# A hybrid encoder layer: mixer work emitted by an estimated clock of each engine, and modulation weights asked for three tiles ahead in four buffers

## The chip, the core and the metric

The kernel runs on one core of one Trainium2 chip. The metric is the device time of one execution in microseconds (us), lower is better. The core has five engines with instruction queues of their own, each worked off in order: TensorE (PE in the profile, with its weight loads as PEld), VectorE (DVE), ScalarE (ACT), GpSimd (POOL) and SyncE (SP), which here issues nearly all DMAs. The kernel is written in a tile framework: the Python code emits instructions in some order, and the framework turns that order, with priorities, into the order of each engine's queue and adds the semaphores. So the order in which the Python code emits is what the programmer controls.

## What is computed

One layer of a streaming encoder in float32 on 512 prompt frames and 64 sample frames, width 2048. Each step is matrix products with large weights, with small recurrent work between:

```python
mod = silu(c) @ w_ada + b_ada                        # 2048 -> 6 x 2048: sh1, sc1, g1, sh2, sc2, g2
h = rmsnorm(x, norm1) * (1 + sc1) + sh1
proj = h @ w_in                                      # split into columns of two groups of heads
o_a = GLA(q, k, v, low-rank gate)                    # 4 heads: S_t = diag(a_t) S_{t-1} + k_t v_t^T
o_b = GDN(silu(conv4(q, k, v)), beta, alpha)         # 8 heads: S_t = a_t (I - b_t k_t k_t^T) S_{t-1} + b_t k_t v_t^T
x = x + g1 * (concat(norm(o_a) * silu(r), norm(o_b) * silu(g)) @ w_out)
h = rmsnorm(x, norm2) * (1 + sc2) + sh2
x = x + g2 * (silu(conv3(gate) + b) * val) @ w_down  # gate, val = h @ w_up
y = rmsnorm(x, final_norm)
```

Each recurrence is evaluated in blocks; for GDN a block needs the inverse of a unit lower triangular matrix, `(eye + lower)`. The states of the recurrences and convolutions are outputs too.

## The kernel before

Products in float32 are made of three passes over a high and a low part of weight and activation (`split` makes the parts on ScalarE, L662, and VectorE, L663; `mm6` is the six matmuls of one 128-row tile for two halves of the frames, L565 and L567).

The stages are: `head` (norms, the first two modulation parts, some early projections), the mixer stage, the rest of `w_out`, `up`, `down`. The change lies in the mixer stage. There the main stream is a sequence of projection tiles (`in_tile`: 16 times `mm6`), 31 for the GDN heads and 19 for the GLA heads, followed by half of `w_out` (16 tiles of 8). After each `mm6` comes one `tick`, 928 in all. A tick does three things:

- `run_due` runs what was put off by a count of ticks (`later`);
- `job_step` resumes the jobs, Python generators in a list: `gdn` for each of eight heads and for the samples, `gla` for each of four heads and for the samples. It goes through them in order and stops after the first that emitted something; a job that says WAIT only lets a tick pass;
- with a rate of `ADA_RATE` = 0.72 a tick it resumes `ada_blocks`, which computes the other four modulation parts: 16 blocks of 8 weight tiles (512 KB each, loaded by L900), each tile four VectorE operations (L938), and at the end of a block a small sum on TensorE (`ada_sum`, L910).

A job has to leave time between an instruction on one engine and the next instruction that needs its result on TensorE, because TensorE's queue is in order: what is emitted too early makes it stand. Before, this time is a fixed count of ticks for each place (`rest(REST_S)`, `hop` with two ticks of rest, `LAG_CONV`, `LAG_COPY` for results of convolutions and copies). The steps that the prediction names:

- `gdn` computes decays (ScalarE; GpSimd `affine_select`), sums of squares and their `rsqrt` (VectorE add L151, GpSimd power), `a` = masked k k^T (L228), and then calls `inverse16`: it stores `a` to DRAM (L373), loads its 16x16 diagonal blocks onto 32 partitions (L379), inverts them with 28 GpSimd operations (listed under L1812, the helper that records GpSimd's operations), stores the result (L390), loads it spread out (L394) and masks it on VectorE (L399). Then come the levels that build the inverse up (matmuls L250, L256, L265, L270, each with a VectorE operation after it), and four blocks of states (L288 to L317). Operations of jobs on VectorE and ScalarE carry the line L1797 of their helper, which gives them a precedence of 80 places.
- `gla` has seven levels (L442 and operations around it), a transpose, and four blocks (L479 to L485).
- `gdn_conv` runs the short convolution (L1073 to L1083); its results are transposed in jobs (L158).
- `ada_blocks` has three buffers `aw` and asks for a tile two tiles ahead.

Buffers named `m` are a common pool of 15. `xr` is a pair of buffers used at the start for the first projection and constants of `narrow`, and later for the loads of `w_out`'s stage. `K.drain()` emits what is left of the jobs after the first half of `w_out`, and the loop behind it what is left of the modulation.

Of the kernel before, what the change touches and what calls it, by code (L numbers as in the profile page):

```python
# [16 lines left out]
P = 128  # L17
# [85 lines left out]
class Kern:  # L103
    def __init__(self, tc, ctx, i, o):
        self.tc, self.nc, self.ctx, self.i, self.o = tc, tc.nc, ctx, i, o
        self.n = 0
        self.cp = ctx.enter_context(tc.tile_pool(name="cp", bufs=1, side="left"))
        self.pg = ctx.enter_context(tc.tile_pool(name="pg", bufs=2, space=PSUM))
        self.c, self.scrap = {}, []
        self.jv, self.ja = _Sooner(tc, tc.nc.vector), _Sooner(tc, tc.nc.scalar)  # L110
        self.pool = _InTurn(tc, tc.nc.gpsimd)
# [37 lines left out]
    def rsqrt(self, out, src, n, parts=P):  # L149

        self.nc.vector.tensor_scalar_add(out[:parts, :n], src[:parts, :n], EPS)  # L151
        self.pool.tensor_tensor(out[:parts, :n], out[:parts, :n], self.mhalf[:parts, :n], op=ALU.pow)

    def transpose4(self, src4, n=4):

        ps = self.bank()
        for b in range(n):
            self.nc.tensor.transpose(ps[:, b * P:(b + 1) * P], src4[:, b], self.c["ident"])  # L158
# [10 lines left out]
    def gdn(self, qF, kF, x, gain, hcols, gb, s0, s_out, o_put, last_level):  # L169
# [11 lines left out]
        V, A, T = self.jv, self.ja, nc.tensor  # L181
# [4 lines left out]
        yield from self.rest(REST_C)  # L186
# [12 lines left out]

# [7 lines left out]

        self.rsqrt(kt[:, 0], ss, 4)
# [3 lines left out]
        V.tensor_tensor(kt[:, 1], kt[:, 1], nbeta, op=ALU.mult)  # L212
        for b in range(4):
            A.activation(dl[:, b], dl[:, b], AF.Copy, scale=kt[:, 1, b:b + 1])
        yield
# [4 lines left out]
        self.rsqrt(rq, ss, 4)  # L220
        V.tensor_scalar_mul(rq, rq, float(P) ** -0.5)
        yield from self.rest(REST_T)


# [6 lines left out]

# [42 lines left out]
        while not self.ready(x, "v"):  # L274
            yield WAIT
# [7 lines left out]
        for b in range(4):  # L283
            parts = [(0, P, st)] if not pair else [(0, 64, s0[2 * b]), (64, P, s0[2 * b + 1])]
            if parts[0][2] is not None:
# [5 lines left out]
                yield from self.hop(0)  # L291
# [6 lines left out]
            yield from self.hop(0)  # L298
# [20 lines left out]
            yield from self.hop(0)  # L319
# [7 lines left out]
        self.rsqrt(rr, ss, 4)  # L327
        for b in range(4):
            A.activation(ops[:, b], ops[:, b], AF.Copy, scale=rr[:, b:b + 1])
        yield from self.rest(REST_N)  # L330
        fps = self.transpose4(ops)
        A.activation(kF, fps, AF.Copy, scale=gain)
        while not self.ready(x, "gate"):
            yield WAIT
        V.tensor_tensor(kF, kF, x["gate"](), op=ALU.mult)
        yield from self.rest(REST_O)
        o_put(kF)

    def ready(self, x, name):

        return name in x and self.ticks >= x.get((name, "at"), 0)

    def put_ready(self, x, name, get, lag):

        x[name], x[name, "at"] = get, self.ticks + lag
# [7 lines left out]
    def rest(self, n):  # L353

        for _ in range(n):
            yield WAIT

    def hop(self, n=REST_H):

        yield  # L360
        yield from self.rest(n)

    def inverse16(self, a, work):
# [16 lines left out]
        yield from self.rest(REST_D)  # L380
# [8 lines left out]
        yield from self.rest(REST_S)  # L389
        nc.sync.dma_start(d1.rearrange("w q f -> q w f"), lane)  # L390
        yield from self.rest(REST_L)
# [4 lines left out]
        yield from self.rest(REST_X)  # L396
        t, u = self.m4(), self.m4()
        for w, x in enumerate((t, u)):
            nc.vector.tensor_tensor(x.rearrange("p b (n j) -> p b n j", n=8), cm[:, w].unsqueeze(2).to_broadcast(sh),  # L399
                                    c["bd16"].rearrange("p (n j) -> p n j", n=8).unsqueeze(1).to_broadcast(sh), op=ALU.mult)  # L400
        yield from self.rest(REST_U)
        return u, t

    def gla(self, nb, qF, kF, g, x, s0, s_out, o_put):
# [7 lines left out]
        V, A, T = self.jv, self.ja, nc.tensor  # L412
        pair = s0 is not None
        w = nb * P
        at = self.m()[:, :w].rearrange("p (b t) -> p b t", b=nb)
# [5 lines left out]
        for s in LEVELS:  # L421
# [10 lines left out]
            A.activation(e, e, AF.Exp, scale=1.0 / 16.0)  # L432
            e3 = e.rearrange("p (b t) -> p b t", b=nb)
# [5 lines left out]
            yield from self.rest(REST_G)  # L439
            ps = self.bank()  # L440
            for b in range(nb):
# [8 lines left out]
        A.activation(qd, g, AF.Exp, scale=1.0 / 16.0)  # L450
        V.tensor_tensor(qd, qd, qF, op=ALU.mult)
# [5 lines left out]
                        gs[:, :, seg - 1:seg].to_broadcast([P, nseg, seg]), gs, op=ALU.subtract)  # L457
        A.activation(kd, kd, AF.Exp, scale=1.0 / 16.0)
        kd3 = kd.rearrange("p (b t) -> p b t", b=nb)
# [4 lines left out]
        yield  # L464
        yield from self.rest(REST_V)
        A.activation(kT, self.transpose4(kd3, nb), AF.Copy)
        yield from self.hop()
        while not self.ready(x, "v"):
            yield WAIT
# [4 lines left out]
        for b in range(nb):  # L474
# [22 lines left out]
            if b % 2 == 1:  # L497
                self.rsqrt(rr[:, b - 1:b + 1], ss[:, b - 1:b + 1], 2)
                V.tensor_tensor(ons[b // 2], ops, self.col4(rr[:, b - 1:b + 1], 256), op=ALU.mult)
            yield  # L500
        if not pair:
            nc.sync.dma_start(s_out, st)
        yield from self.rest(REST_N)
        for f in range(2):
# [4 lines left out]
            yield  # L509
        for f in range(2):  # L510
            dst = (qd, kd3)[f]
            while not self.ready(x, f"gate{f}"):
                yield WAIT
            V.tensor_tensor(dst, dst, x[f"gate{f}"](), op=ALU.mult)
        yield from self.rest(REST_O)
# [4 lines left out]
    def later(self, n, f):  # L520

        self.due.append((self.ticks + n, f))

    def run_due(self):
        while self.due and self.due[0][0] <= self.ticks:
            self.due.pop(0)[1]()

    def tick(self):

        self.ticks += 1  # L530
        self.run_due()
        self.at_job += JOB_RATE
# [3 lines left out]
        self.at_ada += ADA_RATE  # L536
        while self.at_ada >= 1:
            self.at_ada -= 1
            next(self.ada, None)

    def job_step(self):
        for g in list(self.jobs):
            r = next(g, self)
            if r is self:
                self.jobs.remove(g)
# [3 lines left out]
    def drain(self):  # L549
        while self.jobs:  # L550
            self.ticks += 1
            self.run_due()
            self.job_step()
# [1322 lines left out]
```

## Time and profile before

| | |
|---|---|
| runs | 2917.21, 2911.84, 2914.27 us; median 2914.27 |
| profiled execution | 2915.48 us, of which span 2913.8 us |
| TensorE busy in the span | 2823.6 us (97%) |
| mixer stage | about 186 to 1125 us |
| TensorE busy in 186 to 1125 us | 894.1 of 939.0 us |
| granted TensorE clock, mean of the span | 0.985 of full |

The profile is of one execution. Busy time of TensorE is modelled at its end, so it tells where TensorE stood still rather than how fast it was. The row of a group or wait gives the line, the engine, tiles (out<-in), a count, and times; "idle before" is the time an engine stood still ahead of such an instruction and what ended it. A line can be that of a helper (L1797 for VectorE and ScalarE in jobs, L1812 for GpSimd).

### The profile page before, as it was taken

Reading aid. Unit: us, or ns where it says so; the run is one execution under the profiler, and the core shown is the slowest. Engines: PE = TensorE matmul, PEld = TensorE weight load, DVE = VectorE, ACT = ScalarE, POOL = GpSimd, SP = SyncE. Lnnn points to the kernel's source line nnn. Section 1 sums busy time; section 2 is a strip of 40 time slices with the busy share of each in tenths; the row PEclk is TensorE's granted clock in tenths of the full one; section 3 lists DMA queues with packets and bytes.
Section 4 is the critical chain, followed back from the end, with each engine's and each line's share of the span. In section 5 each row is a group of like instructions: output and inputs, shape, how many; then the busy total and the mean of one; then the engine's idle time right before and its main releaser. Section 6 shows DMA issues by size and latency. Waiting matters only on the chain.

```text
span 2913.8 us, 52011 instructions
## 1 busy us (share of the span) xinstructions
PE 2823.6 (97%) x20964; PEld 2739.5 (94%) x20964; DVE 2055.0 (71%) x3305; ACT 1183.4 (41%) x2030; POOL 306.1 (11%) x513
## 2 busy tenths in 40 slices
PE   6997989999899999999999999999999999999998
PEld 3787989999899998999999999999999999999997
DVE  3467667777568687578888888888888855555555
ACT  4143544555454343255444444444444522222223
POOL 0004141222200000000111111111111100000000
PEclk8998999999899999999999999999999999999999
DMA  8965444555445548633333333333333563333221
GB/s 301 307 173 154 138 134 138 152 155 159 132 122 150 150 128 229 181 115 97 115 108 101 107 103 114 108 100 107 108 110 107 165 201 97 119 98 117 83 82 66
DMA packets 535444, 395.53 MB, mean 136 GB/s; under 512 B 59657, under 2 KB 465412, under 8 KB 535204
## 3 DMA queue, kind: packets, MB, share of 16 engines
q1 hardware_dynamic: 527860, 390.54, 44.8%
q8 instruction: 165, 2.70, 0.4%
q10 hardware_dynamic: 7344, 1.67, 0.3%
q14 instruction: 75, 0.61, 0.1%
HBM read 356.47 MB, written 35.67 MB: 135 GB/s over the span
## 4 chain that ended last, share of the span: by engine, by line
PE 83%; DVE 6%; POOL 3%; issue 2%; DMA 2%; ACT 2%; SPq 0%; ACTq 0%; POOLq 0%; DVEq 0%
PE g L565 28%; PE g L567 14%; PE bank L1476 12%; PE bank L1475 11%; PE bank L1477 11%; POOL m L1812 2%; DVE acc L938 2%; PE bank L754 1%; PE bank L158 1%; PE bank L442 1%; DVE m L1797 1%; DVE wl L663 1%; DVE ca L1078 1%; ACT m L1797 0%; PE bank L256 0%
## 5 line engine op out<-in xcount | busy, mean ns | idle before, releaser
L1476 PE MATMUL bank<-slot,wh 128*128 128x290 f32 x2464 | 738.7, 300 | 0.0
L1475 PE MATMUL bank<-slot,wh 128*128 128x290 f32 x2464 | 734.7, 298 | 0.0
L1477 PE MATMUL bank<-slot,wl 128*128 128x290 f32 x2464 | 728.4, 296 | 0.0
L565 PE MATMUL g<-slot,wh 128*128 128x288 f32 x3168 | 551.4, 295 | 0.3 <-DVE slot L1245 0.3
L565 PE MATMUL g<-hh,wh 128*128 128x288 f32 x2048 | 478.6, 314 | 1.3 <-ACT wh L662 0.8
L1477 PEld LDWEIGHTS bank<-slot,wl 128*128 128x128 f32 x2464 | 471.5, 191 | 0.0
L1476 PEld LDWEIGHTS bank<-slot,wh 128*128 128x128 f32 x2464 | 468.5, 190 | 0.1
L565 PEld LDWEIGHTS g<-slot,wh 128*128 128x128 f32 x3168 | 464.1, 188 | 0.7 <-DVE slot L1245 0.5
L1475 PEld LDWEIGHTS bank<-slot,wh 128*128 128x128 f32 x2464 | 463.6, 188 | 0.1
L662 ACT ACTIVATE wh<-raw 128x1024 fp32r<-128x1024 f32 x215 | 227.6, 1059 | 538.5 <-PE g L565 513.7
L565 PE MATMUL g<-hl,wh 128*128 128x288 f32 x2048 | 444.9, 298 | 0.0
L567 PE MATMUL g<-hh,wl 128*128 128x288 f32 x2048 | 443.4, 298 | 0.0
L1245 DVE SCALAR_TENSOR_TENSOR slot<-g,mod,slot 128x512 f32<-128x512 f32 (+1 forms) x448 | 201.6, 491 | 263.8 <-PE g L567 262.7
L565 PEld LDWEIGHTS g<-hh,wh 128*128 128x128 f32 x2048 | 329.8, 192 | 25.5 <-issue 14.9
L938 DVE SCALAR_TENSOR_TENSOR acc<-aw,ct,acc 128x512 f32<-128x512 f32 x480 | 337.1, 748 | 19.5 <-DMA aw<-in_w_ada_dram 19.5
L567 PE MATMUL g<-slot,wl 128*128 128x288 f32 x1584 | 341.9, 294 | 0.0
L565 PEld LDWEIGHTS g<-hl,wh 128*128 128x128 f32 x2048 | 333.7, 191 | 3.6 <-issue 2.7
L567 PEld LDWEIGHTS g<-hh,wl 128*128 128x128 f32 x2048 | 331.0, 190 | 2.2 <-issue 2.0
L663 DVE TENSOR_TENSOR wl<-raw,wh 128x1024 fp32r<-128x1024 f32 x215 | 262.5, 1221 | 65.1 <-ACT wh L662 64.4
L1422 ACT ACTIVATE wh<-raw 128x1024 fp32r<-128x1024 f32 x176 | 186.1, 1057 | 224.8 <-PE bank L1476 189.5
L567 PEld LDWEIGHTS g<-slot,wl 128*128 128x128 f32 x1584 | 255.5, 188 | 0.0
L1423 DVE TENSOR_TENSOR wl<-raw,wh 128x1024 fp32r<-128x1024 f32 x176 | 215.2, 1223 | 54.8 <-ACT wh L1422 54.8
(355 smaller groups left out, 3101.0 us busy)
## 6 DMA issues: line engine op xcount, KB each, us to landing
raw<-in_w_up_dram SPq DMA_DIRECT2D x176, 512.0 KB
aw<-in_w_ada_dram SPq DMA_DIRECT2D x128, 512.0 KB
raw<-in_w_in_dram SPq DMA_DIRECT2D x100, 512.0 KB
raw<-in_w_down_dram SPq DMA_DIRECT2D x88, 512.0 KB
hraw<-in_w_ada_dram SPq DMA_DIRECT2D x64, 512.0 KB
raw<-in_w_out_dram SPq DMA_DIRECT2D x32, 512.0 KB
slot<-actd SPq DMA_DIRECT2D x44, 288.0 KB
actd<-v SPq DMA_DIRECT2D x44, 256.0 KB
```

The costliest lines, as they stand in the source:

```text
L565: T.matmul(ps[:, h if bank is None else bank, :n], wh, x[:, h, :n], start=f, stop=False)
L567: T.matmul(ps[:, h if bank is None else bank, :n], wl, ah[:, h, :n], start=False, stop=stop)
L662: nc.scalar.activation(hi[:, :n_], raw[:, :n_], AF.Copy)
L663: nc.vector.tensor_tensor(lo[:, :n_], raw[:, :n_], hi[:, :n_].bitcast(F32), op=ALU.subtract)
L938: V.scalar_tensor_tensor(acc[s], w[:, k], col, acc[s], op0=ALU.mult, op1=ALU.add)
L1245: self.nc.vector.scalar_tensor_tensor(x1[:, :, z], ps[:, :, c], gain[:, q:q + 1], x1[:, :, z], op0=ALU.mult, op1=ALU.add)
L1422: self.nc.scalar.activation(hi, src, AF.Copy)
L1423: self.nc.vector.tensor_tensor(lo, src, hi.bitcast(F32), op=ALU.subtract)
L1475: T.matmul(ps, wh[:, j], hi, start=(c < 3 and j == 0), stop=False, skip_group_check=True)
L1476: T.matmul(ps, wh[:, j], lo, start=False, stop=False, skip_group_check=True)
L1477: T.matmul(ps, wl[:, j], hi, start=False, stop=(j == NPAIR - 1), skip_group_check=True)
L1812: r = f(*a, **kw)
```

## The change

The ticks are replaced by a running estimate of time. `now` advances by `TICK_US` with each tick and by a fixed price for each TensorE instruction of a job. Every instruction of the stage on VectorE, ScalarE and GpSimd goes through a wrapper that adds its estimated duration to that engine's `free` time, and a job's own `chain` is the estimated end of its last step. A job waits until `now` has passed `chain` plus `HOP_US`. GpSimd's estimate has longer durations than the other two, and an extra for the power in `rsqrt`; a DMA counts `DMA_US` plus `ISSUE_US` for each transfer. Convolutions and the GLA gate become generators of their own (`tasks`), run at each tick. The modulation goes on as long as VectorE's estimated backlog is under `ADA_BACKLOG`; its waits don't use up its rate. Its tiles are asked for three ahead, in two buffers `aw` and the two `xr` in turn, but only one ahead and in `aw` alone from the last GLA head on (`ending`). The pool `m` has 17 buffers. Sample jobs and GLA jobs wait until at most one `gdn` job of a head is left (`fewer`).

```diff
-REST_S, REST_L, REST_D, REST_X, REST_U, REST_T, REST_H, REST_N, REST_O, REST_G = 2, 3, 6, 4, 12, 2, 2, 4, 4, 4
-REST_C = 11
-REST_V = 5
-LAG_CONV, LAG_COPY = 11, 5
-ADA_AHEAD = 2
+TICK_US, HOP_US, DMA_US, ISSUE_US = 0.795, 0.25, 2.6, 0.5
+ADA_BACKLOG, ADA_CREDIT = 1.0, 200.0
+OP_US = {"V": (0.12, 1 / 960.0), "A": (0.10, 1 / 960.0), "G": (0.45, 1 / 400.0)}
+ADA_AHEAD = 3
...
     def rsqrt(self, out, src, n, parts=P):
-        self.nc.vector.tensor_scalar_add(out[:parts, :n], src[:parts, :n], EPS)
+        self.tv.tensor_scalar_add(out[:parts, :n], src[:parts, :n], EPS)
         self.pool.tensor_tensor(out[:parts, :n], out[:parts, :n], self.mhalf[:parts, :n], op=ALU.pow)
+        self.slower("G", 0.7)
+    def rsqrt_steps(self, out, src, n):
+        self.rsqrt(out, src, n)
+        yield from self.until()
...
+    def charge(self, key, n, extra=0.0):
+        base, per = OP_US[key]
+        start = max(self.free[key], self.now + HOP_US, self.chain or 0.0)
+        self.free[key] = end = start + base + per * n + extra
+        if self.chain is not None:
+            self.chain = end
+    def charge_pe(self, us):
+        self.now += us
+        if self.chain is not None:
+            self.chain = max(self.chain, self.now)
+    def until(self):
+        while self.now < self.chain + HOP_US:
             yield WAIT
-    def hop(self, n=REST_H):
+    def hop(self):
         yield
-        yield from self.rest(n)
+        yield from self.until()
+    def moved(self, n=1):
+        self.chain = max(self.chain, self.now) + DMA_US + n * ISSUE_US
...
     def inverse16(self, a, work):
-        yield from self.rest(REST_S)
+        yield from self.until()
         nc.sync.dma_start(d0[:P * pitch].rearrange("(p f) -> p f", p=P), a.rearrange("p b t -> p (b t)"))
-        yield from self.rest(REST_L)
+        self.moved()
+        yield from self.until()
...
         for b in range(4):
             nc.sync.dma_start(xx[8 * b:8 * b + 8], blocks[:, :, b, :16])
-        yield from self.rest(REST_D)
+        self.moved(4)
+        yield from self.until()
...
         G.tensor_copy(xt, xx.rearrange("p i j -> p j i"))
-        yield from self.rest(REST_S)
+        yield from self.until()
         nc.sync.dma_start(d1.rearrange("w q f -> q w f"), lane)
-        yield from self.rest(REST_L)
+        self.moved()
+        yield from self.until()
...
-        yield from self.rest(REST_U)
+        yield from self.hop()
         return u, t
...
     def tick(self):
-        self.ticks += 1
+        self.now += TICK_US
         self.run_due()
+        self.run_tasks(list(self.tasks))
         self.at_job += JOB_RATE
         while self.at_job >= 1:
             self.at_job -= 1
             self.job_step()
-        self.at_ada += ADA_RATE
-        while self.at_ada >= 1:
+        self.at_ada = min(self.at_ada + ADA_RATE, ADA_CREDIT)
+        while self.at_ada >= 1 and self.free["V"] - self.now < ADA_BACKLOG:
+            r = next(self.ada, self)
+            if r is self or r is WAIT:
+                break
             self.at_ada -= 1
-            next(self.ada, None)
...
     def ada_blocks(self, blocks, accs):
-            while len(got) < min(len(todo), n + 1 + ADA_AHEAD):
-                got.append(self.ada_load(*todo[len(got)], lambda: self.ap.tile([P, 1024], F32, tag="aw", bufs=1 + ADA_AHEAD, name=self.name("aw"))))
+            while len(got) < min(len(todo), n + 1 + (1 if self.ending else ADA_AHEAD)):
+                j = len(got)
+                own = lambda: self.ap.tile([P, 1024], F32, tag="aw", bufs=2, name=self.name("aw"))
+                got.append(self.ada_load(*todo[j], self.xr if j % 2 and not self.ending else own))
                 if n == 0:
-                    yield
+                    yield WAIT
...
             if k0 + 2 == KD:
-                yield from self.rest(4)
+                yield from self.pause(self.free["V"] + HOP_US)
                 yield from self.ada_sum(blk, acc)
...
     def gdn_conv(self, ps, t, dst, name, h, done):
         A.activation(acc[:, :579], cb[:, 0:579], AF.Copy, scale=self.vec("gdn_conv_w", t))
+        yield from self.until()
         for j in range(1, 4):
             V.scalar_tensor_tensor(acc[:, :579], cb[:, j:j + 579], self.vec("gdn_conv_w", 24 * j + t), acc[:, :579],
                                    op0=ALU.mult, op1=ALU.add)
+        yield from self.until()
         A.activation(dst, acc[:, 0:512], AF.Silu)
+        done(end + HOP_US)
...
+class _Timed:
+    def __getattr__(self, name):
+        f = getattr(self.engine, name)
+        def g(*a, **kw):
+            out = kw["out"] if "out" in kw else a[0]
+            self.k.charge(self.key, _size(out), 0.2 if "accum_out" in kw else 0.0)
+            return f(*a, **kw)
+        return g
+class _TimedPE:
+    def transpose(self, out, *a):
+        self.k.charge_pe(0.11)
+        return self.engine.transpose(out, *a)
+    def matmul(self, out, *a, **kw):
+        self.k.charge_pe(0.22 * max(1.0, _size(out) / P))
+        return self.engine.matmul(out, *a, **kw)
...
-    BUFS = {"m": 15, "qkv": 8, "gt": 3}
+    BUFS = {"m": 17, "qkv": 8, "gt": 3}
```

In `gdn` and `gla` every `rest` and fixed `hop` becomes `until` or `hop`, and every wait for a convolution, copy or gate becomes `wait_for` an estimated time.

More of the change, by code (lines that the diff above doesn't have):

```diff
@@ L290, in gdn @@
                 rhs = r
-                yield from self.hop(0)
+                yield from self.hop()
             else:
@@ L549, in drain @@
     def drain(self):
-        while self.jobs:
-            self.ticks += 1
+        while self.jobs or self.tasks:
+            self.now += TICK_US
             self.run_due()
+            self.run_tasks(list(self.tasks))
             self.job_step()
@@ L1183, in gla_gate @@
             A.activation(t, t, AF.Ln, bias=one[:, 0:1])
+        self.slower("A", 2.6)
+        yield from self.until()
         for z, t, c0, n, seg in parts:
```

262 lines of the change are left out of this document (167 added, 95 removed).

## The prediction

> **What bounds the kernel now.** I read the page first (sections 1 and 4), then a table of windows over the mixer stage, then the list of what TensorE waited for, and last the timeline around one long gap.
>
> ```profile
> PE 2823.6 (97%) x20964; PEld 2739.5 (94%) x20964; DVE 2055.0 (71%) x3305; ACT 1183.4 (41%) x2030; POOL 306.1 (11%) x513
> PE 83%; DVE 6%; POOL 3%; issue 2%; DMA 2%; ACT 2%; SPq 0%; ACTq 0%; POOLq 0%; DVEq 0%
> 186.00:1125.00 939.00, 894.08 (x6704) 859.45 (x6703) 685.92 (x1307) 447.87 (x1035) 185.38 (x341) 0.97 0.52 148
> 437.00:729.00 292.00, 284.67 (x2217) 277.09 (x2216) 216.41 (x395) 146.81 (x371) 72.51 (x131) 0.99 0.53 151
> ```
>
> In the last two rows the columns are PE, weight load, DVE, ACT and POOL busy, then granted clock, DMA share and GB/s. TensorE bounds the kernel. The change only reorders the mixer stage (186 to 1125 us), where TensorE idles 939.0 - 894.1 = 45 us and the clock is below full. No TensorE instruction is removed, so idle time and clock there are all that can be won. The steady GDN heads (437 to 729) lose only 292.0 - 284.7 = 7 us; the losses are in single events.
>
> ```profile
> PE bank L256 <- POOL m L1812: 11.7, 2, 7.8
> PE bank L256 <- DVE m L1797: 9.3, 4, 7.5
> PE bank L250 <- DVE m L399: 6.0, 2, 3.2
> PE bank L158 <- ACT qkv L1082: 5.0, 2, 2.5
> PE bank L158 <- ACT qkv L1219: 3.3, 1, 3.3
> PE bank L270 <- DVE m L1797: 2.1, 1, 2.1
> ```
>
> Each row is total us, times, longest. The waits are few and long: the inverse levels L250, L256 and L270, and transposes waiting for a late convolution (L1082). One event in order of time shows how they arise:
>
> ```profile
> 264.29 16.14 POOL L1812 TENSOR_TENSOR m<-m 32x14 f32<-32x14 f32 x28
> 264.85 0.38 SPq L900 DMA_DIRECT2D aw<-in_w_ada_dram  x1
> 281.11 0.33 SPq L390 DMA_DIRECT2D d<-m  x1
> 281.48 0.42 SPq L900 DMA_DIRECT2D aw<-in_w_ada_dram  x1
> 285.64 0.75 DVE L938 SCALAR_TENSOR_TENSOR acc<-aw,ct,acc 128x512 f32<-128x512 f32 x1 [9.32 <-DMA aw<-in_w_ada_dram]
> 286.31 0.41 DVE L1797 TENSOR_TENSOR m<-bank,consts 128x256 f32<-128x256 f32 x1
> 286.88 1.94 PE L256 MATMUL bank<-m,m 128*128 128x64 f32 x8 [7.54 <-DVE m L1797]
> SPq L390 <- POOL m L1812: 85.3, 9, 15.7
> SPq L900 <- DVE acc L938: 229.4, 82, 11.5
> ```
>
> POOL works 16 us on a GDN inverse. Its result store (L390) stands at the head of SP's queue meanwhile, the next modulation tile behind it is asked for only at 281.48, DVE waits 9.3 us for that tile, and the level's own DVE operation stands behind. TensorE gets the bill. The store blocks SP in all nine jobs, 9.5 us each.
>
> The clock adds to it (PE busy, clock, DMA share, GB/s):
>
> ```profile
> 260.00:263.30 3.30, 3.30 (x26) 1.00 0.19 40
> 286.90:288.50 1.60, 1.60 (x8) 0.50 0.98 328
> 288.50:292.60 4.10, 4.10 (x19) 0.50 1.09 316
> 757.90:763.00 5.10, 5.10 (x23) 0.50 0.51 121
> ```
>
> After the 7.5 us gap TensorE works 5.7 us at half clock and loses 2.85; after the 3.3 us gap 5.1 us, losing 2.55. The 2.8 us wait at L250 just before 260 cost no clock. So a long gap costs its length and about 2.7 us more. [...]
>
> **The change part by part.**
>
> *Waits by the clock.* Fixed counts of ticks give way to waits until an estimated end. The gain is where counts went wrong: a `rsqrt` on POOL queued behind another job's inverse now enters the estimate, so DVE is no longer given work that blocks at its head, and the store L390 is emitted when POOL should be done. The estimate for one inverse is 28 operations at 0.45 us plus size/400 (15.4), memset 0.5 and copy 1.1: 17.0 us.
>
> ```profile
> L1812 POOL TENSOR_TENSOR m<-m 32x14 f32<-32x14 f32 (+6 forms) x252 | 115.1, 457 | 18.6
> 530.36 1.64 DMA d<-m
> 532.06 2.69 DMA cm<-d
> ```
>
> Measured: 28 x 0.457 = 12.8 us plus the copy, so the estimate is generous on average. The two DMA steps behind it are estimated at 3.1 + 3.6 = 6.7 us and took 4.4: some 2.3 us in hand, plus rounding to ticks. The waits this addresses are L256, L250, L270 and L158 from L1082: 11.7 + 9.3 + 6.0 + 2.1 + 5.0 = 34.1 us. Bounds of the gain: 34 if all go, 17 if half move to the next hop, since POOL's work itself is not shortened. I take nine tenths, 31, because all of these go back to late POOL, SP or DVE order, which the clock tracks. The 3.3 us (L1219, ACT) I leave. Four of these gaps are long (7.8 and 3.9 in the first row, 7.5, 3.2): 4 x 2.7 = 11 us of clock (0 to 14).
>
> *Shorter hops.* Before, a hop is three ticks (2.4 us at the 0.795 that the change's own constant gives a tick). After, it is the first tick past the estimated end plus 0.25 us, mostly two. About 24 hops in each of nine `gdn` jobs and 15 in each of five `gla` jobs make 290. What a hop loses today:
>
> ```profile
> PE bank L442 <- DVE m L1797: 0.7, 1, 0.7
> PE bank L295 <- DVE sq L1797: 0.5, 1, 0.5
> PE bank L507 <- DVE m L1797: 0.5, 1, 0.5
> L663 DVE TENSOR_TENSOR wl<-raw,wh 128x1024 fp32r<-128x1024 f32 x34 | 41.8, 1229 | 6.8 <-ACT wh L662 6.5 <-DMA qkv<-early_aq 0.2
> L1797 ACT ACT_TABLE_LOAD x18 | 23.1, 1283 | 0.7 <-ACT ts L1236 0.4
> ```
>
> Almost nothing: single waits of 0.5 to 0.7 us. With the slack cut, a hop behind a 1.23 us weight split can wait for part of it. Lower bound 0; upper 290 x 0.2 = 58 us, each hop waiting half of its own 0.41 us operation. I take 0.04 us, nearer to today's rows: one hop in fifteen waits 0.6. That is +12.
>
> *Modulation pace.* Rests no longer cost steps: 16 blocks x 32 = 512 steps at 0.72 a tick end after 711 ticks of 928, not 915.
>
> ```profile
> L938 DVE SCALAR_TENSOR_TENSOR acc<-aw,ct,acc 128x512 f32<-128x512 f32 x150 | 105.2, 746 | 0.0
> 437.00:729.00 292.00, 199.93 (x1082) 158.08 (x1082) 0.99 0.53 151
> 437.00:729.00 292.00, 116.28 (x541) 86.82 (x540) 0.99 0.53 151
> 1000.00:1210.00 210.00, 63.95 (x92) 0.99 0.58 166
> ```
>
> The first two window rows (L565 and L567 alone) give (1082 + 541)/6 = 270 ticks, 284.7/270 = 1.05 us of TensorE each. DVE without L938 is (216.4 - 105.2)/270 = 0.41 us a tick; 0.72 steps of 0.70 us add 0.50. DVE goes from 74% to 0.91/1.05 = 87%. The last row is L938 alone: 92 steps still run after 1000 us today, and these move forward, where nothing waits for them but DVE's own queue. DVE stays under the bound, the emission stops at 1 us of estimated backlog, and the hop price above is what I charge for it. From head 3 only one tile is asked ahead; 704 x 0.72 = 507 steps are then done, so a tile or two may wait: +0.5.
>
> *Four buffers, three ahead.* A load still waits on SP for the last operation on the tile before (the L900 row), so SP's blocking there stays. Cover rises from two tiles to three, 12 steps or 17 ticks, against the 16 us that SP was shut in the event above: that is what hides a late store. Two of the buffers are `xr`; the second such load waits for `narrow`'s constants, with weight loads behind it: 0 to 3 us once, I take 0.5.
>
> *POOL against DVE.* A busier DVE may slow POOL:
>
> ```profile
> 264.29 5.73 POOL L1812 TENSOR_TENSOR m<-m 32x14 f32<-32x14 f32 x5
> 264.00:270.00 6.00, 2.71 (x12) 2.74 (x13) 6.00 (x11) 0.00 (x0) 5.46 (x6) 0.64 0.95 275
> 485.16 4.85 POOL L1812 TENSOR_TENSOR m<-m 32x14 f32<-32x14 f32 x14
> 485.00:490.00 5.00, 5.00 (x41) 5.00 (x40) 0.81 (x2) 0.39 (x1) 3.88 (x15) 1.00 0.76 215
> 692.46 7.99 POOL L1812 TENSOR_TENSOR m<-m 32x14 f32<-32x14 f32 x12
> ```
>
> With DVE busy 6.0 of 6 us in modulation sums an operation took 1.15 us, with DVE nearly idle 0.35; at 692, among mixed work, 0.67. At 0.70 an inverse takes 19.6 + 0.7 = 20.3 us, 3.3 over the estimate; 2.3 and the tick rounding absorb nearly all. I charge 0.3 us in nine jobs: +3 (0 to 77, below). [...]
>
> The sum, against the profiled execution's 2915.5 us (span 2913.8 and 1.7 outside): 2915.5 - 31 - 11 + 12 + 1 + 3 = 2889.5. The median of the runs is 1.2 us lower: **2888 us**.
>
> **The rivals.** *All waits go, hops are free.* 2914.3 - 34.1 - 3.3 - 14 = 2863. For it: small waits hardly exist now. Against: slack is what keeps them away.
>
> *Hops without slack.* The steady heads lose 7 us in 292 now; a mean wait of 0.2 us a hop costs 58, so 2914.3 - 42 + 58 + 4 = 2934, slower. It decides from 38/290 = 0.13 us a hop. For it: DVE at 87%, ACT's table loads of 1.28 us that the estimate leaves out. Against: the backlog gate, and the mixers' instructions keep their precedence.
>
> *POOL outlasts its estimate.* At 0.9 us an operation the inverse takes 25.9 us, 5.9 late past all cover, and with 2.7 of clock 8.6 x 9 = 77: 2914.3 - 42 + 12 + 1 + 77 = 2962, slower. From about 0.85 it decides. Against: 0.67 was the mean at the busiest place among mixed work.
>
> *The order hardly changes.* L390 used to come 16 ticks (16.8 us) after POOL's start and the estimate for an undisturbed inverse is 17.0: if other jobs' POOL work matters little, gains and hop waits cancel, 2909 to 2920.
>
> **How the numbers follow.** Forecast as summed, 2872 to 2905: 0.55. All waits go: 0.15. Hops without slack: 0.17. POOL outlasts: 0.06. No change: 0.07. About 0.2% (6 us) is what a measurement of this kernel can tell from no change. Faster 0.70, same 0.07, slower 0.23. The range, 2860 to 2930, takes in the first two cases and the milder part of the slower ones.
>
> **What would show it.** Right: the SP wait at L390 far under 85 us, no DVE wait of 9 us for `aw`, the waits at L256 and L250 mostly gone, no half clock after an inverse; no L938 left after 1000 us, against 92 now; DVE near 87% in the GDN heads. Wrong: many new waits of 0.3 to 1 us at L250, L256, L295, L301 and L442 that sum above 40 us, or POOL operations near 0.9 us with DVE blocked at L399 for `cm`.

## The result, and the profile after

The changed kernel takes 2893.15 us (median of four runs, 2890.08 to 2895.03) against 2913.97 us for the kernel before on the same chip: a ratio of 0.9923, 95% interval 0.9911 to 0.9935, 20.8 us faster. The profiled execution took 2892.92 us (span 2890.8, mean clock 0.987), 22.6 us less than that of before. The forecast was 2888.

The page, busy time of each engine and the chain that ended last:

```profile
PE 2811.7 (97%) x20964; PEld 2733.9 (95%) x20964; DVE 2059.6 (71%) x3305; ACT 1185.4 (41%) x2031; POOL 330.1 (11%) x513
PE 87%; DVE 3%; DMA 3%; POOL 3%; issue 2%; ACT 1%; SPq 0%; ACTq 0%; POOLq 0%; DVEq 0%
```

The same work, with less of the chain that ended last outside TensorE (13% against 17%). The windows of the mixer stage (PE, weight load, DVE, ACT, POOL busy, clock, DMA share, GB/s):

```profile
186.00:1125.00 939.00, 906.42 (x6909) 876.70 (x6908) 726.88 (x1371) 456.79 (x1048) 208.36 (x341) 0.98 0.55 159
437.00:729.00 292.00, 271.92 (x2084) 264.65 (x2084) 216.87 (x391) 136.47 (x347) 88.20 (x143) 0.96 0.56 161
```

In the same 939 us TensorE now gets through 6909 matmuls, not 6704, and idles 32.6 us, not 44.9. But 437 to 729, which had lost 7 us, loses 20 now. What TensorE waited for between 186 and 1125 us (total, times, longest):

```profile
PE bank L1947 <- ACT sq L1907: 11.3, 2, 10.3
PE bank L1947 <- DVE conv_in L1931: 6.8, 2, 4.5
PE g L641 <- ACT wh L1931: 4.4, 1, 4.4
PE bank L1947 <- DVE st L1907: 3.4, 1, 3.4
PE bank L1947 <- DVE sq L1907: 2.5, 4, 1.0
PE bank L1943 <- ACT qkv L1931: 1.6, 1, 1.6
PE bank L1947 <- DVE m L1907: 1.2, 1, 1.2
PE bank L1947 <- DVE m L1931: 0.8, 1, 0.8
```

The wrappers have lines of their own: matmuls of jobs are L1947, transposes L1943, `mm6` L641 and L643, VectorE and ScalarE L1907 (jobs) and L1931 (others), GpSimd L1961, the inverse's store L430, its reload L435. The waits for `m`, once 29.1 us at L256, L250 and L270, are down to 2.0. New ones have come, 28.4 us in the first five rows, and one gap of 10.3 us holds a third of that. What VectorE waited for from DMA, before (first fence) and after (second):

```profile
DVE m L399 <- DMA cm<-d: 21.0, 4, 9.0
DVE acc L938 <- DMA aw<-in_w_ada_dram: 19.5, 5, 9.3
```

```profile
DVE acc L1931 <- DMA aw<-in_w_ada_dram: 8.7, 3, 7.3
DVE m L1931 <- DMA cm<-d: 0.4, 1, 0.4
```

The first of these four rows was not in the prediction: before, VectorE stood 21.0 us at the head of its queue for the inverse's reload `cm`, beside 19.5 us for modulation tiles. The clock takes the first to 0.4. A third wait, which the prediction names without a row, is that for a `rsqrt` that GpSimd does only after another job's inverse; it holds 6.7 us in one place before and 1.1 at most after (first row before, second after):

```profile
DVE kt L1797 <- POOL kt L1812: 14.3, 8, 6.7
DVE kt L1907 <- POOL kt L1961: 8.3, 9, 1.1
```

By the order in VectorE's queue before, TensorE's long waits come behind all three: 6.8 us (ended at 259.86 and 267.29) behind the `rsqrt`, 15.4 us (286.88 and 417.28) behind late tiles, 10.3 us (539.64, 609.21, 787.23 and 792.19) behind `cm`. The two waits at L256 that the profile puts down to POOL are among them: VectorE's own operation of that level ended 0.15 us before each of them did, at 267.14 and 417.13.

SP's wait at the inverse's store, and the inverse's own operations (the fence of groups):

```profile
SPq L430 <- POOL m L1961: 109.6, 9, 20.6
```

```profile
L1961 POOL TENSOR_TENSOR m<-m 32x14 f32<-32x14 f32 (+6 forms) x252 | 140.2, 556 | 18.4
```

Both rose: SP's wait from 85.3 to 109.6 us, a GpSimd operation from 457 to 556 ns.

The one long gap, in order of time (timeline of the changed kernel; start, length, engine, line):

```profile
697.92 20.49 POOL L1961 TENSOR_TENSOR m<-m 32x14 f32<-32x14 f32 x28
701.65 0.38 SPq L976 DMA_DIRECT2D aw<-in_w_ada_dram  x1
719.09 0.32 SPq L430 DMA_DIRECT2D d<-m  x1
722.26 0.86 SPq L1230 DMA_DIRECT2D out_dram<-sq  x2
726.10 0.26 ACT L1931 ACTIVATE sq<-sq 128x64 f32<-128x64 f32 x1 [14.03 <-DMA out_dram<-sq]
728.35 0.26 ACT L1907 ACTIVATE sq<-bank 128x128 f32<-128x128 f32 x1
728.66 1.23 PE L1947 MATMUL bank<-sq,m 128*128 128x128 f32 x4 [10.32 <-ACT sq L1907]
```

SP stood from 702 to 719 at the store. A store of convolution state (L1230) lay behind it; the buffer `sq` that it empties had been given to the GLA gate, so ScalarE stood 14 us for it, with the copy that TensorE needed behind.

### The profile page after: what moved, and what is told of

It reads as the page before. It is cut to its first block, busy times and chain, and to the rows that moved or that the text cites. A ratio compares the mean times of both kernels' runs of the same rounds, so it can differ in the third digit from the quotient of the medians.

```text
span 2890.8 us, 52029 instructions
## 1 busy us (share of the span) xinstructions
PE 2811.7 (97%) x20964; PEld 2733.9 (95%) x20964; DVE 2059.6 (71%) x3305; ACT 1185.4 (41%) x2031; POOL 330.1 (11%) x513
## 3 DMA queue, kind: packets, MB, share of 16 engines
q1 hardware_dynamic: 527860, 390.54, 44.9%
## 4 chain that ended last, share of the span: by engine, by line
PE 87%; DVE 3%; DMA 3%; POOL 3%; issue 2%; ACT 1%; SPq 0%; ACTq 0%; POOLq 0%; DVEq 0%
PE g L641 29%; PE g L643 14%; PE bank L1584 12%; PE bank L1583 11%; PE bank L1585 11%; PE bank L1947 5%; POOL m L1961 3%; PE bank L1943 1%; DVE acc L1931 1%; PE bank L830 1%; DVE wl L1931 1%; DMA m<-gd 0%; ACT m L1907 0%; DMA raw<-in_w_in_dram 0%; PE ps_nar L1050 0%
## 5 line engine op out<-in xcount | busy, mean ns | idle before, releaser
L641 PE MATMUL g<-slot,wh 128*128 128x288 f32 x3168 | 551.6, 295 | 0.3 <-DVE slot L1931 0.3
L641 PE MATMUL g<-hh,wh 128*128 128x288 f32 x2048 | 474.7, 313 | 5.4 <-ACT wh L1931 4.4
L641 PEld LDWEIGHTS g<-slot,wh 128*128 128x128 f32 x3168 | 464.2, 188 | 0.7 <-DVE slot L1931 0.5
L1931 ACT ACTIVATE wh<-raw 128x1024 fp32r<-128x1024 f32 x215 | 227.6, 1059 | 545.5 <-PE g L641 537.6
L641 PE MATMUL g<-hl,wh 128*128 128x288 f32 x2048 | 443.4, 298 | 0.0
L643 PE MATMUL g<-hh,wl 128*128 128x288 f32 x2048 | 443.2, 298 | 0.0
L1931 DVE SCALAR_TENSOR_TENSOR slot<-g,mod,slot 128x512 f32<-128x512 f32 (+1 forms) x448 | 201.7, 491 | 304.2 <-PE g L643 303.0
L641 PEld LDWEIGHTS g<-hh,wh 128*128 128x128 f32 x2048 | 328.4, 191 | 28.4 <-issue 14.2
L643 PE MATMUL g<-slot,wl 128*128 128x288 f32 x1584 | 342.1, 295 | 0.0
L641 PEld LDWEIGHTS g<-hl,wh 128*128 128x128 f32 x2048 | 332.9, 190 | 3.4 <-issue 2.5
L643 PEld LDWEIGHTS g<-hh,wl 128*128 128x128 f32 x2048 | 330.9, 190 | 2.4 <-issue 2.4
L1931 DVE TENSOR_TENSOR wl<-raw,wh 128x1024 fp32r<-128x1024 f32 x215 | 262.5, 1221 | 28.1 <-ACT wh L1931 25.1
L643 PEld LDWEIGHTS g<-slot,wl 128*128 128x128 f32 x1584 | 255.5, 188 | 0.0
L1530 ACT ACTIVATE wh<-s 128x1024 fp32r<-128x1024 f32 x132 | 140.2, 1062 | 210.5 <-DVE s L1541 109.2
```

Of the source, the lines that this page charges most:

```text
L641: T.matmul(ps[:, h if bank is None else bank, :n], wh, x[:, h, :n], start=f, stop=False)
L643: T.matmul(ps[:, h if bank is None else bank, :n], wl, ah[:, h, :n], start=False, stop=stop)
L1530: self.nc.scalar.activation(hi, src, AF.Copy)
L1931: return f(*a, **kw)
```

## The experiments

All are compared with the kernel before on the same chip (its medians were 2914.0 to 2916.4 us). "Work" is the matmuls that TensorE got through in 186 to 1125 us, "idle" the time in it that TensorE was not busy, "cm" and "aw" VectorE's waits for the reload and for the modulation tile (in `aw` or `xr`) there, "op" the mean GpSimd operation of the inverse in ns.

| kernel | median us | ratio | work | idle us | cm | aw | op |
|---|---|---|---|---|---|---|---|
| before | 2914 | 1 | 6704 | 44.9 | 21.0 | 19.5 | 457 |
| changed | 2893.2 | 0.9923 | 6909 | 32.6 | 0.4 | 8.7 | 556 |
| 1 e2, before + buffers | 2914.9 | 1.0003 | 6710 | 47.6 | 42.0 | 2.6 | 461 |
| 2 e10, before, store off SP | 2912.6 | 0.9993 | 6777 | 41.9 | 38.8 | 4.0 | 461 |
| 3 e6, changed, store off SP | 2892.4 | 0.9925 | 6894 | 35.2 | 0 | 5.6 | 557 |
| 4 e1, changed, two ahead | 2894.4 | 0.9931 | 6899 | 32.8 | 1.6 | 8.5 | 557 |
| 5 e3, changed, short GpSimd | 2877.9 | 0.9872 | 6980 | 22.2 | 1.4 | 0 | 501 |
| 6 e19, short operation alone | 2888.3 | 0.9904 | 6905 | 27.8 | 1.2 | 7.0 | 506 |
| 7 e5, state store off SP | 2887.5 | 0.9909 | 6930 | 28.3 | 0 | 7.4 | 552 |
| 8 e14, e3 and e5 | 2876.8 | 0.9871 | 7011 | 19.6 | 1.3 | 0 | 503 |
| 9 e4, shorter hops | 2889.3 | 0.9915 | 6901 | 26.4 | 0.6 | 4.3 | 406 |
| 10 e20, e14 and shorter hops | 2928.2 | 1.0039 | 6635 | 55.3 | 34.3 | 1.4 | 531 |
| 11 e16, store and reload off SP | 2915.5 | 1.0002 | 6720 | 43.0 | 7.7 | 0.5 | 538 |
| 12 e8, slower modulation | 2882.3 | 0.9882 | 6955 | 25.1 | 0 | 8.1 | 548 |

**1. The buffers alone**, on the kernel before: two `aw`, two `xr`, three ahead (one ahead from the last GLA head on, as in the change).

```diff
-ADA_AHEAD = 2
+ADA_AHEAD = 3
-  ... "aw", bufs=1 + ADA_AHEAD
+  ... self.xr if j % 2 and not self.ending else own      # own: "aw", bufs=2
```

> The kernel before with the four modulation buffers alone: two aw and the two xr in turn, asked for three tiles ahead, one ahead from the last GLA head. If late modulation tiles are what stops TensorE (theory A: a longer lead hides the store that blocks SP), the DVE wait for aw (19.5 us) goes and with it the 7.5 and 7.8 us waits at L256 and their half clock: 2890 to 2900. If the tiles are late only because a job's work is emitted at the wrong time (theory B: the clock is what matters), the DVE wait shrinks but TensorE waits at L250 and L256 stay for other reasons: 2905 to 2914.

2914.86 us, ratio 1.0003 (0.9994 to 1.0012): nothing, as in theory B. Yet VectorE's wait for tiles is all but gone:

```profile
DVE m L399 <- DMA cm<-d: 42.0, 8, 9.8
DVE acc L940 <- DMA aw<-in_w_ada_dram: 2.6, 2, 2.3
```

The 17 us came back at another operation. The sums no longer stand, so VectorE gets sooner to the mask L399, whose `cm` comes when GpSimd is done and not before: 40.5 us of the two waits before, 44.6 now. The late tile was a symptom.

**2 and 3. The inverse's store from GpSimd's queue**, in the kernel before and in the changed one.

```diff
-        nc.sync.dma_start(d1.rearrange("w q f -> q w f"), lane)
+        nc.gpsimd.dma_start(d1.rearrange("w q f -> q w f"), lane)
```

> The kernel before with this store alone moved to GpSimd's queue. If SP standing at that store is the root of the long waits in the kernel before, as the prediction has it for one event, the waits at L256 and L158 mostly go: 2885 to 2900. If GpSimd's order and DVE blocked at rsqrt are the root, the 2.8, 3.9 and one of the 7.8 us waits stay: 2903 to 2912.

> The changed kernel with the inverse's result stored from GpSimd's own queue in place of SP's, so that nothing stands behind it on SP. If SP's blocking (109.6 us at L430 in the profile after) still costs TensorE there, the 10.3 us wait for the sq buffer, whose earlier store stands behind L430, and part of the 4.5 and 3.4 us waits go: 2872 to 2882. If those waits come from DVE or GpSimd being late themselves, little changes: 2888 to 2896. GpSimd's own issue adds some tenths of a us per job.

2912.63 us, 0.9993 (0.9984 to 1.0002), and 2892.44 us, 0.9925 (0.9912 to 0.9937): nothing in either. In the first, the tile wait again turns into a wait for `cm` (19.5 to 4.0, 21.0 to 38.8), and the waits of TensorE that its second theory names stay: 2.8, 3.9 and 7.8 us became 3.7, 2.4 and 6.4. So does VectorE's wait for the `rsqrt` behind an inverse (7.5 us in one place). In the second, the reload behind the store takes over its place on SP, which reached L1230 only at 722.95, and TensorE's gap was 10.55 us.

**4. Two tiles ahead**, in the four buffers.

```diff
-ADA_AHEAD = 3
+ADA_AHEAD = 2
```

> The changed kernel with its four modulation buffers, but asked for two tiles ahead instead of three. If three ahead is needed to cover a late store on SP: DVE's wait for aw rises from 8.7 us to some 20 us and the time by 5 to 10 us, 2898 to 2903. If it is not: within 3 us of 2893, as the buffers alone gave nothing.

2894.35 us, 0.9931 (0.9918 to 0.9945), 1.2 us from the changed kernel and inside both intervals; the tile wait is the same 8.5 us. The depth does nothing that can be measured here. Whether the wait fell from 19.5 to 8.7 by the clock's order or by the four buffers under it was not separated.

**5 and 6. Short GpSimd estimates:** as short as VectorE's and without the extra behind `rsqrt`, then the operation's duration alone.

```diff
-OP_US = {..., "G": (0.45, 1 / 400.0)}
+OP_US = {..., "G": (0.12, 1 / 960.0)}
-        self.slower("G", 0.7)                # left in experiment 6
```

> The changed kernel with GpSimd's estimate cut to VectorE's (0.12 us plus size/960 and no extra for the power): one inverse counts as about 5 us, where it takes 13 to 26. Theory B says the long estimate carries the gain: the store is emitted some 12 us too early, SP stands at L430 for over 20 us a job, TensorE waits at the inverse levels come back, 2910 to 2940. If the gain is in the other waits and the buffers (theory A), it stays within 2888 to 2900.

> The changed kernel with only the duration of a GpSimd operation short (0.12 us and size/960), and the 0.7 us behind each rsqrt kept. Both short took 2877.9 us. If the inverse's estimate is what costs (its 14 ticks of emission are a floor of about 11 us, the estimate adds 6): within 3 us of 2878. If it is the rsqrt chains (four in each gdn job, 0.7 us each in the chain of its own head): above 2885.

The first misses its expectation by a sign: 2877.94 us, 0.9872 (0.9859 to 0.9886), 15 us better than the changed kernel. The long estimates cost. The second, 2888.29 us (0.9904, 0.9891 to 0.9918), splits that: about 5 us for the operation's duration (its interval still touches that of the changed kernel), 10 for the extra in the `rsqrt` chains. A likely reason, not tested by itself, is that the inverse's loop yields at 14 places, which already spreads its emission over some 11 us; experiment 10 shows that the slack of the hops is needed then. VectorE waited 1.4 us for `cm`.

**7 and 8. Convolution-state stores from ScalarE's queue**, in the changed kernel and with the short estimates.

```diff
-            nc.sync.dma_start(o["ps"[s] + "_conv"]...
+            nc.scalar.dma_start(o["ps"[s] + "_conv"]...
```

> The changed kernel, with the convolution-state stores (L1230) issued by ScalarE's queue instead of SP's. Theory A (one event: the state rows sit on SP behind the inverse's store, and a gla_gate sum that takes over their sq buffer waits 10.3 us for them): the gap of 10.3 us at L1947 and some 2.6 us of half clock behind it go, so about 12 us less than the changed kernel, near 2880 us; SP's wait at L430 stays near 110 us. Theory B (the long GpSimd estimate itself delays the heads, wherever the wait then lands): another wait takes its place and the time stays within 5 us of 2893 us.

> The changed kernel with a GpSimd estimate as short as VectorE's and without the 0.7 us added after each rsqrt, and with the convolution-state stores from ScalarE's queue. The short estimate alone took 2877.9 us. Theory A (the two act on the same 10.3 us event): no more than 3 us better than 2877.9. Theory B (the estimate's length costs by itself and the event by itself): the gains add, near 2866 us.

2887.46 us, 0.9909 (0.9895 to 0.9923): 5.7 us less than the changed kernel, half of theory A's 12, with intervals that overlap. The wait for `sq` is still there, shorter:

```profile
PE bank L1947 <- ACT sq L1907: 7.1, 2, 6.2
```

ScalarE now waited 11.0 us for another buffer held by the same late inverse (`m`, read by its store). With the short estimates too: 2876.8 us, 0.9871 (0.9857 to 0.9884), 1.1 us better than the short estimates alone, which is noise. So the two do not add, and the trace of experiment 5 shows why: with the short estimates TensorE has no wait for `sq` from ScalarE left. The inverse ends there at 706 us, and the state rows are stored at 713. Experiment 8 has the lowest median of all, 16 us under the changed kernel.

**9 and 10. Shorter hops**, with the long estimates and with the short ones (and the state store of 7).

```diff
     def until(self):
-        while self.now < self.chain + HOP_US:
+        while self.now < self.chain - 0.4:
```

> The changed kernel, with each wait by the clock ended 0.65 us earlier (0.4 us ahead of the estimated end instead of 0.25 us behind it): less slack in every hop. The prediction's hop term (0.04 us in each of 290 hops, more with less slack): small waits of 0.2 to 0.6 us at the inverse levels rise by 20 us or more, 2910 us and over. If hops have slack to spare: within 5 us of 2893 us, or faster as the long chains end sooner.

> The changed kernel with the short GpSimd estimates, the state stores on ScalarE's queue and each wait by the clock ended 0.65 us earlier. Short estimates and state stores alone took 2876.8, the shorter waits alone gained 4. If slack in the hops is surplus: 2870 to 2874. If the estimates' length was the slack that covered the hops (both taken away leave none): many new waits of 0.3 to 1 us at the inverse's levels, 2885 us or more.

With the long estimates 2889.29 us, 0.9915 (0.9901 to 0.9929): 4 us less by the median, with overlapping intervals, so hops had slack to spare. With the short ones 2928.22 us, 1.0039 (1.0026 to 1.0053), 51 us worse than experiment 8 and slower than the kernel before. VectorE's waits in the second:

```profile
DVE m L1930 <- DMA cm<-d: 34.3, 8, 8.9
```

and one of these events in order of time:

```profile
544.61 0.62 POOL L1960 COPY m<-m 32x256 f32<-32x256 f32 x1
545.25 0.33 SPq L429 DMA_DIRECT2D d<-m  x1
546.91 0.92 SPq L434 DMA_DIRECT2D cm<-d  x2
550.02 0.69 DVE L1930 TENSOR_TENSOR m<-cm,consts 128x512 f32<-128x512 f32 x1 [6.62 <-DMA cm<-d]
550.63 0.16 DVE L1930 TENSOR_SCALAR kt<-s 128x4 f32<-128x4 f32 x1
550.87 1.38 POOL L1960 TENSOR_TENSOR kt<-kt,mhalf 128x4 f32<-128x4 f32 x1 [5.64 <-DVE kt L1930]
```

The mask was emitted too early for its reload, and VectorE stood at it with everything behind it. It worked that off until 562.63, when it came to the level's own operation, and TensorE stood for it from 555.07 to 563.19. There are four such pieces of up to 8.6 us (the profile names a later operation on VectorE, `rq`):

```profile
PE bank L1946 <- DVE rq L1930: 29.2, 4, 8.6
```

This is the wait of the kernel before, and more of it. Either the long estimates or the 0.65 us of slack covers the inverse. Having both costs some time (2893 against 2877 to 2889 us), having neither costs far more (2928).

**11. Store and reload from GpSimd's queue** (the reload in two pieces).

```diff
-        nc.sync.dma_start(d1...)
+        nc.gpsimd.dma_start(d1...)
-            nc.sync.dma_start(cm[:, w], ...)
+            for b in (0, 2):
+                nc.gpsimd.dma_start(cm[:, w, b:b + 2], ...)
```

> The changed kernel with both the inverse's store (L430) and its reload (L435, in two pieces per half) issued by GpSimd's own queue, so that nothing of the inverse's end stands on SP. Theory 1 (SP shut for 110 us in nine pieces is what makes heads late: a decays load behind it held ScalarE for 13.1 us, a state store TensorE for 10.3): the gaps of 4.5 us (conv_in) and 10.3 us (sq) go, with 2 x 2.7 us of clock behind them, 15 to 20 us better than 2893, near 2875. Theory 2 (TensorE waits for the inverse's result or the mixer chain itself, and SP only carries the name): another 5 us or less, or slower by the longer issue of the reload.

2915.49 us, 1.0002 (0.9993 to 1.0011), 22 us worse than the changed kernel. The waiting moved to GpSimd's queue, where the `rsqrt` of other heads stand behind the reload; VectorE's wait for them, against 8.3 us in nine:

```profile
DVE kt L1908 <- POOL kt L1962: 34.2, 9, 11.9
```

This answers neither theory cleanly, as it puts a new wait in place of the one it takes away. Part of that is the longer issue that theory 2 mentions: GpSimd spent 0.73 us on each of the reload's 36 issues, where SP spent 0.42 (median) on each of its 18 in the changed kernel, and stood 63.2 us ahead of 28 of them for nothing else that the trace shows. What it shows is that GpSimd's queue is, by these 22 us, a worse place for the pair in this kernel than SP's.

**12. Slower modulation:** 0.62 steps a tick.

```diff
-JOB_RATE, ADA_RATE = 1.0, 0.72
+JOB_RATE, ADA_RATE = 1.0, 0.62
```

> The changed kernel with the modulation's pace at 0.62 steps a tick instead of 0.72, so that VectorE does fewer sums beside each GpSimd inverse. If the sums are what slows GpSimd's operations (457 ns before, 556 ns after): their mean falls to 0.50 us or below, and SP's wait at L430, which has been the inverse's operations less 28 to 31 us in every run, falls from 110 to about 96 us. If that is also what costs TensorE time: 5 us or more below 2893. If the inverse's speed is not on TensorE's path: within 4 us of 2893, or later by the sums that move to the stage's end.

The GpSimd operation is as slow as before (548 ns, SP's wait 108.0 us), and the reason shows in the sums that VectorE did in the GDN heads, in the changed kernel and here (windows of the tile `acc`; VectorE busy, clock):

```profile
437.00:729.00 292.00, 118.28 (x169) 0.96 0.56 161
```

```profile
437.00:729.00 292.00, 116.82 (x167) 0.96 0.55 161
```

The lower rate hardly changed them (0.62 a tick by itself would give 159 in the 256 ticks there), so it is not the rate that sets the pace, and whether fewer sums would speed up GpSimd's operations was not tested. The time fell all the same, to 2882.28 us, 0.9882 (0.9866 to 0.9899): 11 us. The wait of 4.4 us for `wh` is gone and the one of 10.3 is 6.5. Why these moved was not shown; an order that differs a little meets other single events.

## Why the prediction was right, point by point

**Waits by the clock** (forecast -31). Right in size: the five groups named and the one left (L1219), 37.4 us, fell to 3.6. Its reason was half right. That a `rsqrt` behind another job's inverse would no longer stop VectorE came true (6.7 us at most before, 1.1 after), and neither the moved store nor the buffers alone remove it (7.5 and 5.9 us in experiments 2 and 1). But the one event that the prediction followed led it to the late modulation tile. Experiments 1 and 2 take most of that tile wait away and gain nothing, as VectorE then stands as long for `cm`: fixed counts brought the mask to it before the reload could be there. Under the clock that wait is gone (21.0 to 0.4 us), and in experiment 10, with less estimate and slack, both the wait and the time are back. Experiment 10 shortens every hop, so it does not show this for the mask alone.

**"The store L390 is emitted when POOL should be done."** Wrong in effect. SP's wait at the store was to be far under 85 us and is 109.6. In every run with the store on SP that wait follows the time of the inverses' 252 operations, less 20 to 35 us over nine inverses: 115.1 and 85.3 before, 140.2 and 109.6 after, 102.4 and 73.8 in experiment 9. So SP gets to the store 2 to 4 us after the inverse begins on average, whatever the estimate (at 702 for the inverse of 697.92 above). The likely reason, which no run isolates: nothing holds SP to the clock, and what is emitted later is still reached as soon as the loads ahead of it have their buffers.

**The clock of TensorE** (-11). Right in direction, with a smaller size: half-clock records in the mixer stage sum to 51.2 us before and 30.7 after. Of these TensorE worked 37.8 and 21.5 us, the rest lay in the gaps themselves; with half of that work counted as lost, as the prediction does, the loss fell from 18.9 to 10.8 us, by 8. And 2.7 us a gap is no constant (below). The prediction's two rows stop short of the records, which end at 292.99 and 764.03: TensorE worked 6.1 us at half clock after both gaps.

**Shorter hops** (+12). The sum needed a loss of about this kind, and the mechanism was wrong. The new waits are not 0.6 us in one hop of fifteen; they are ten, 28.4 us in all, half of it in two of 10.3 and 4.5 us. Experiment 9, with still less slack, is no slower. So the term should have been about zero for slack, and some 28 for new collisions.

**Closing the sum.** Waits between 186 and 1125 us were 44.5 us and are 32.5: 33.8 gone from the named groups, 6.6 from the small ones, 28.4 new. With 8 us of clock that is -20, and the profiled executions differ by 22.6; the other 2.5 us were not traced. That the forecast of 2888 lies 5 us from the result is in part luck: the loss of 12 us that it set against its gains came, but larger (28.4, less 6.6 from small waits) and for another reason, and the clock gave 8 and not 11.

**Modulation pace.** Wrong in size. VectorE in the GDN heads is busy 216.9 of 292 us, 74% as before, not 87%, and 34 operations of the sums run after 1000 us, not none (98 before). In the GDN heads 169 are done against 160 before, where 0.72 a tick would be about 183 (254 ticks there after). Experiment 12 shows that the rate is not what binds; the backlog gate is the likely one, but that was not tried. So the hop price lost its cause too.

**Four buffers, three ahead** (+0.5). Its small price was right; "that is what hides a late store" was not. Experiment 1 finds no gain in the buffers alone, experiment 4 none in the third tile under the clock.

**POOL against DVE** (+3). The row was read rightly, and operations slowed, by 25 us over nine inverses. That TensorE would pay little holds for most of them; the place at 698 us, 20.5 us for an inverse against an estimate of 17.0, is in the 10.3 us gap. Taking the long estimates as useful cover was the larger error: with the hops as they are they cost 15 us (experiment 5), about 5 of it for the durations behind the 17.0 (experiment 6).

**The rivals.** "All waits go, hops are free" (2863) did not come about: old waits went almost all, and new ones took their place. Experiment 8 gets half of the way there, to 2877. "POOL outlasts its estimate" did not come about here, but its mechanism, VectorE blocked for `cm`, is that of the kernel before and of experiment 10. By that run, what decides is not 0.85 us an operation, but how much estimate and slack together stand behind it: experiment 10 has 0.53.

**The signs.** Of what was to show the prediction right, the waits at L256 and L250 went, and no wait of 9 us for `aw` is left (7.3 at most). Four signs failed: SP's wait at the store rose, sums ran after 1000 us, VectorE was at 74%, and a half clock of 10.2 us stands behind the inverse of 697.92. So the time was forecast better than the way to it.

**Left open.** Of the 15 us that the long estimates cost, a large part is the event at 718 us: in the profiled executions, 11.8 us apart, TensorE's idle time falls by 10.4 us, and of its waits the 11.3 us for `sq` and the 4.4 for `wh` are gone, with new ones of 4.7 and 3.5 us. Why the extra behind `rsqrt` weighs twice the durations was not traced. No run took out the 17 buffers of `m`, the convolutions as tasks or the wait of `fewer` one by one; they stay in experiment 10, so they do not make the gain without the margins, but their share in it is not known. That variants of the same clock lie 4 to 11 us apart for edits that should matter little (experiments 9 and 12) says that this much depends on which events meet.

## What to carry to other kernels

When a blocked engine's wait is taken away, look which operation stands behind it in the queue and whether its own input will be there; here a tile loaded in time only moved VectorE's wait to `cm`. An estimated clock helped here with what VectorE was given to do (its wait for `cm` fell from 21.0 to 0.4 us); it did not delay the queue that issues the DMAs, which ran ahead (SP's wait at the store rose from 85.3 to 109.6 us). Slack in a planner was needed once: try the estimates short and the margins long, and the other way round, before adding both.

## What the runs showed of the hardware

In both traces a GpSimd operation of the inverse took about 2.6 times as long in the mean wholly beside a VectorE TENSOR_TENSOR or SCALAR_TENSOR_TENSOR as beside none: after, 71 operations beside none took 0.257 us in the mean and 114 wholly beside them 0.656; before, 113 took 0.255 and 99 took 0.665. So the mean of 457 or 556 ns went with what VectorE did at that place, not with its work in total: in experiment 9 VectorE is as busy as in the changed kernel (725.0 and 726.9 of 939 us), and the mean is 406. No run changed this alone, so the cause was not shown. Two stretches, the first of experiment 9 and the second of the changed kernel (PE, weight load, DVE, ACT, POOL busy, clock):

```profile
658.30:669.00 10.70, 10.70 (x83) 10.70 (x82) 2.02 (x4) 3.19 (x10) 8.90 (x27) 1.00 0.33 96
```

```profile
697.00:718.40 21.40, 21.33 (x162) 19.91 (x160) 17.83 (x30) 6.47 (x16) 18.43 (x29) 1.00 0.27 79
```

With VectorE busy 2.0 of 10.7 us, GpSimd did 27 operations in 8.9 us; with 17.8 of 21.4, it needed 18.4 for 29.

In the mixer stage of the two traces the half clock after a gap lasted by its records 3.4, 6.8 or 10.2 us, and how much of that fell on work differed (changed kernel; TensorE busy, clock):

```profile
728.66:732.20 3.54, 3.54 (x15) 0.50 0.31 111
556.08:561.60 5.52, 5.52 (x25) 0.50 0.50 154
```

After the gap of 10.3 us TensorE worked 3.6 us at half clock (its record ends at 732.26), after that of 4.5 us 5.5 us. With half of that work counted as lost, an estimate as in the prediction, the longer gap cost 1.8 us more than its length, the shorter 2.8. The records show where the difference lies. In the changed kernel the shortest half-clock record is 3.413 us long (from 162.23 us), called a step here. The four of the mixer stage begin at 452.37, 554.77, 722.02 and 1066.76 us, which is 0, 30, 79 and 180 steps from the first, and last 6.83, 6.83, 10.24 and 6.83 us, two or three steps. Counted on in these steps, the gap of 10.3 us ended at 728.66, 0.2 us ahead of the next, and that of 4.5 us at 556.08, 2.1 us ahead of one. In both, the work at half clock was what was left of that step and one whole step more. The two gaps of the prediction ended 2.7 us ahead of a step by the records of the trace before (from 282.76 and 757.21 us), which gives the 6.1 us.

Two shorter gaps of the trace before went different ways: one of 2.5 us (from 606.66) was followed by a step at half clock (610.43 to 613.85), and one of 2.8 us (from 257.03) by none. Of the first, 2.2 us lay in one step; the second lay in two, with 1.8 and 1.0 us. No run varied the length or the place of a gap, so what decides was not shown.
